# A decoder layer: 18 of the 22 gate and up tiles of both SwiGLUs computed in pairs by seven half-size block products

## The chip, the cores and the metric

One NeuronCore of a Trainium2 chip. TensorE (PE) multiplies a weight block of 128 x 128, which it loads first (PEld), with a moving tile of up to 512 columns and adds the products up in a PSUM bank; it has two clocks, 1.2 and 2.4 GHz. VectorE (DVE), ScalarE (ACT) and GpSimd (POOL) work on 128 partitions of SBUF or PSUM; SyncE (SP) issues the DMAs. The metric is the device time of one launch in microseconds, the median over runs.

## The reference

One layer on 512 tokens of 1024 features, all in float32:

```
h = x
h = h + 0.5 * rms(swiglu(rms(h, g1), Wgate1, Wup1, Wdown1), g1post)     # FFN1, d_ff = 2816
u = rms(h, gmix)
proj = u @ w_in                       # inputs of two token mixers and their gates
y_a = sparse latent attention(proj)   # top 128 keys per token, 8 heads
y_b = chunked gated linear recurrence(proj), 4 heads
merged = sigmoid(gate_a) * (y_a @ w_br_a) + sigmoid(gate_b) * (y_b @ w_br_b)
h = h + rms(merged @ w_out, gmixpost)
h = h + 0.5 * rms(swiglu(rms(h, g2), Wgate2, Wup2, Wdown2), g2post)     # FFN2, d_ff = 2816
h = h + rms(sigmoid(rms(h, gple) @ w_ple_gate) * (p @ w_ple_proj), gplepost)

swiglu(x) = (silu(x @ Wgate) * (x @ Wup)) @ Wdown
rms(x, g) = x * rsqrt(mean(x * x) + 1e-6) * g
```

## The kernel before

Activations lie transposed, features on partitions: `h` is 8 blocks of 128 features by 512 tokens. Every product is made in three parts, to keep float32 accuracy: an operand is cast to a shorter float (`hi`, ACT), the rest is `lo` = operand - `hi` (DVE), and PE adds `w_hi x hi`, `w_lo x hi` and `w_hi x lo` into one bank (`mm3_step`, L206 to L209; `matmul`, L239). For the inputs, `prenorm_tile` (L283, L284) writes `hg_hi` and `hg_lo`, which hold `h` times the gain; the factor per token, 1/rms, is left out of the product and multiplied into its result as `R` (`scaled`, L360).

An FFN has 22 tiles of 128 hidden features in `GROUPS` of 8, 7 and 7. For a tile, `weight` fetches 128 x 1024 weights of gate into a `raw` tile by a DMA on SP, and `weight_part` casts (L163, ACT) and subtracts (L165, DVE) into a `w` tile; likewise up. Each of the two products is 8 blocks of features x 3 parts = 24 matmuls of 512 tokens, into a bank of its own from a ring of eight (`mm`, `pl`, `hg`, `pt`, `po`). `hidden` then multiplies both by `R` on DVE (L360), takes silu on ACT, multiplies the two (L369, DVE) and splits into `hid_hi` (L186, ACT) and `hid_lo` (L187, DVE). After a group, eight down products use its hidden tiles (`product`): for m of the 8 output blocks, nf x 3 matmuls of 512 into a bank; the first group is copied to `y` (ACT), later ones are added (L413, DVE).

In FFN1 tile 0 is made while x arrives (`begin`). In FFN2 tiles 0 and 1 are computed in two halves of 256 tokens, since the second half's input is ready later. In the last group `last_product` computes the last 4 (FFN1) or 5 (FFN2) down blocks in token halves too, so that `residual` of the first half (post norm, sum, next pre-norm) runs beside the products of the second. Tiles are allocated from rings (`raw` 3, `w` 6, `t` 4 deep), and a scheduler orders each engine's instructions by estimated times; the kernel is otherwise written in program order.

POOL adds squares for the norms (L277), takes a few weight splits and parts of the mixers. In the gate and up products it has nothing to do.

## Time and profile before

| | us |
|---|---|
| median of 3 timed runs (lowest, highest) | 1249.57 (1249.42, 1252.25) |
| the profiled execution, its own time | 1253.45 |
| its span in the profile | 1251.7 |
| PE, DVE, ACT, POOL busy in the span | 1223.0, 710.7, 531.7, 297.7 |
| mean granted clock of PE (1 is the higher level) | 0.997 |

The stages, in us from the start of the span, read off the lines in the trace: FFN1 gate/up of its three groups 5 to 99.7, 143.3 to 220.3 and 258.4 to 334.5, each followed by its down products; residual to about 375; mixers and their input products to 735; merge to 822.6; FFN2 to 1192.8; the last part with the per-layer embeddings to 1251.7. Busy time is the union of an engine's instructions; a matmul's modelled duration overlaps the next one's, so the pitch is read between starts, not from durations.

### The profile page before, as it was taken

How to read it: one execution, taken by the hardware profiler on the slowest of the kernel's cores; microseconds unless marked ns; L12 is line 12 of the kernel's file. 1: busy time of each engine (PE TensorE's matmuls, PEld its weight loads, DVE VectorE, ACT ScalarE, POOL GpSimd, SP SyncE). 2: the span in 40 equal slices, each digit the busy share in tenths (PEclk: the TensorE clock that was granted, in tenths of full speed). 3: DMA queues.
4: the chain of work that ended last, by engine and by line, in shares of the span. 5: the costliest groups of instructions: out<-in, count | busy, mean ns of one | idle time of the engine just before them, and what ended most of it. 6: DMA issues, size and time to landing. Idle time of an engine off the chain costs nothing.

```text
span 1251.7 us, 16612 instructions
## 1 busy us (share of the span) xinstructions
PE 1223.0 (98%) x6263; PEld 1036.9 (83%) x6263; DVE 710.7 (57%) x1252; ACT 531.7 (42%) x909; POOL 297.7 (24%) x348
## 2 busy tenths in 40 slices
PE   7999999999999999999999999989999999999997
PEld 5888888888898888888878887988888888888986
DVE  7543226444448659997766758295532444444386
ACT  6423213222336455555767654364332222222363
POOL 3000000000045203636856622360000000000374
PEclk9999999999999999999999999999999999999999
DMA  6432354333245402423212245223323323332131
GB/s 223 134 94 93 89 107 130 111 101 93 78 129 171 142 21 85 128 89 122 72 55 87 91 146 191 76 85 101 115 87 101 99 88 100 101 95 91 51 152 68
DMA packets 45576, 131.29 MB, mean 105 GB/s; under 512 B 5144, under 2 KB 10424, under 8 KB 45496
## 3 DMA queue, kind: packets, MB, share of 16 engines
q1 hardware_dynamic: 45496, 130.24, 33.4%
q8 instruction: 49, 0.80, 0.3%
q14 instruction: 31, 0.25, 0.1%
HBM read 118.16 MB, written 12.06 MB: 104 GB/s over the span
## 4 chain that ended last, share of the span: by engine, by line
PE 80%; DVE 11%; ACT 3%; DMA 2%; issue 2%; POOL 1%; SPq 0%; DVEq 0%; POOLq 0%; ACTq 0%
PE mm L239 32%; PE pl L239 21%; PE po L239 10%; PE pt L239 9%; DVE hg_lo L284 2%; DVE w L165 2%; DVE h L338 1%; PE po L581 1%; DMA g<-gate_d 1%; DVE z L336 1%; PE hg L705 1%; DVE sc L532 1%; PE pl L560 1%; PE pt L577 1%; DVE small L531 1%
## 5 line engine op out<-in xcount | busy, mean ns | idle before, releaser
L163 ACT ACTIVATE w<-raw 128x1024 fp32r<-128x1024 f32 (+5 forms) x205 | 208.6, 1021 | 384.9 <-PE mm L239 111.7
L239 PE MATMUL mm<-hg_hi,w 128*128 128x512 f32 (+1 forms) x1104 | 339.9, 387 | 0.7 <-DVE small L569 0.7
L165 DVE TENSOR_TENSOR w<-raw,w 128x1024 fp32r<-128x1024 f32 (+5 forms) x189 | 228.6, 1213 | 105.3 <-ACT w L163 103.8
L239 PEld LDWEIGHTS mm<-hg_hi,w 128*128 128x128 f32 x1104 | 203.6, 188 | 40.2 <-DVE w L165 1.1
L277 POOL TENSOR_TENSOR acc<-acc,sq 128x256 f32<-128x256 f32 x78 | 68.0, 876 | 683.9 <-ACT sq L276 682.6
L239 PE MATMUL mm<-hg_lo,w 128*128 128x512 f32 (+1 forms) x552 | 212.6, 387 | 1.3 <-DVE hg_lo L284 1.3
L239 PE MATMUL pl<-hg_hi,w 128*128 128x512 f32 (+1 forms) x592 | 174.2, 377 | 5.3 <-ACT w L163 5.0
L239 PEld LDWEIGHTS pl<-hg_hi,w 128*128 128x128 f32 x592 | 108.8, 191 | 25.6 <-ACT w L163 5.0
L239 PEld LDWEIGHTS mm<-hg_lo,w 128*128 128x128 f32 x552 | 103.5, 188 | 21.3 <-DVE hg_lo L284 1.5
L239 PE MATMUL pl<-hg_lo,w 128*128 128x512 f32 (+1 forms) x296 | 110.3, 376 | 0.7 <-DVE hg_lo L284 0.7
L239 PE MATMUL pt<-hg_hi,w 128*128 128x512 f32 (+1 forms) x256 | 79.2, 388 | 0.8 <-ACT w L163 0.5
L239 PE MATMUL pl<-hid_hi,w 128*128 128x512 f32 (+1 forms) x290 | 79.0, 359 | 0.0
L360 DVE TENSOR_TENSOR t<-mm,R 128x512 f32<-128x512 f32 (+1 forms) x44 | 29.1, 662 | 86.5 <-PE mm L239 65.7
L239 PE MATMUL po<-hg_hi,w 128*128 128x512 f32 (+1 forms) x256 | 77.1, 382 | 0.0
L239 PE MATMUL mm<-hid_hi,w 128*128 128x512 f32 (+1 forms) x278 | 75.3, 357 | 0.0
L239 PEld LDWEIGHTS pl<-hg_lo,w 128*128 128x128 f32 x296 | 56.0, 191 | 10.6 <-DVE hg_lo L284 1.0
L239 PEld LDWEIGHTS pl<-hid_hi,w 128*128 128x128 f32 x290 | 51.7, 189 | 8.1
L239 PEld LDWEIGHTS pt<-hg_hi,w 128*128 128x128 f32 x256 | 47.9, 190 | 11.7 <-ACT w L163 1.0
L239 PEld LDWEIGHTS mm<-hid_hi,w 128*128 128x128 f32 x278 | 49.6, 189 | 7.6
L239 PEld LDWEIGHTS po<-hg_hi,w 128*128 128x128 f32 x256 | 47.5, 188 | 9.4
L360 DVE TENSOR_TENSOR t<-pl,R 128x512 f32<-128x512 f32 (+1 forms) x30 | 20.2, 672 | 58.6 <-PE pl L239 58.5
L239 PE MATMUL pl<-hid_lo,w 128*128 128x512 f32 (+1 forms) x145 | 52.0, 359 | 0.0
(300 smaller groups left out, 2144.4 us busy)
## 6 DMA issues: line engine op xcount, KB each, us to landing
raw<-ffn_w_gate SPq DMA_DIRECT2D x43, 512.0 KB, 3.6
raw<-ffn_w_up SPq DMA_DIRECT2D x43, 512.0 KB, 3.6
raw<-ffn_w_down SPq DMA_DIRECT2D x32, 448.0 KB, 3.3
raw<-ffn_w_down SPq DMA_DIRECT2D x16, 512.0 KB, 3.5
raw<-w_gates SPq DMA_DIRECT2D x16, 512.0 KB, 3.6
gate_d<-t SPq DMA_DIRECT2D x16, 256.0 KB, 2.0
raw<-w_br SPq DMA_DIRECT2D x8, 512.0 KB, 3.2
raw<-w_out SPq DMA_DIRECT2D x8, 512.0 KB, 4.3
```

Of the source, the lines that this page charges most:

```text
L163: hi = nc.scalar.activation(w[:, 0, c], raw[:, c], AF.Copy)
L165: lo = eng.tensor_tensor(w[:, 1, c], raw[:, c], w[:, 0, c].bitcast(F32), op=OP.subtract)
L239: i = self.nc.tensor.matmul(*args, **kw)
L277: eng.tensor_tensor(acc[:, c:c + 256], acc[:, c:c + 256], sq, op=OP.add)
L284: lo = nc.vector.scalar_tensor_tensor(self.hg_lo[:, k, cols], self.h[:, k, cols], g, self.hg_hi[:, k, cols].bitcast(F32), op0=OP.mult, op1 ...
L336: nc.vector.scalar_tensor_tensor(z, y[:, k, c], g[:, k:k + 1], bc, op0=OP.mult, op1=OP.mult)
L338: eng.tensor_tensor(self.h[:, k, c], self.h[:, k, c], z, op=OP.add)
L360: self.nc.vector.tensor_tensor(t, ps, self.R[:, cols], op=OP.mult)
L531: nc.vector.max(best, sc)
L532: nc.vector.match_replace(sc, best, sc, TAKEN)
L560: nc.tensor.matmul(pl, st[:, tok], kh[:, part, :nk], start=(part == 0), stop=(part == 1))
L577: nc.tensor.transpose(pt[:, k], lg[:, k], self.ident)
```

## The change

The weight tiles of nine pairs in each FFN (18 of the 22 tiles) are no longer multiplied one by one. For gate, and for up, the two tiles and the 8 feature blocks, as 2 x 2 blocks (A11, A12: the first tile's weights for the first four and the last four feature blocks; A21, A22: the second tile's), meet the input's 2 x 2 blocks (B: feature halves by token halves) in seven block products of 4 feature blocks x 256 tokens x 3 parts = 12 matmuls each, by the Strassen-Winograd scheme. It needs four sums of input blocks, T1 to T4, made once per FFN (`input_sums`: from `h` times gain, subtractions on POOL, split on ACT and DVE), and four sums of weight blocks per tile pair, S1 to S4 (`pair`: two on POOL, two on DVE, each split on ACT and DVE). Sums of results are made in PSUM where products share a bank (banks "a", "c") and otherwise by a copy out of PSUM (ACT) and an addition (DVE). `R` is multiplied into the gate half on POOL (`gated`) and into the product's second factor on POOL or DVE.

The groups are 6, 4, 6 and 6 tiles; the first has tiles 0 to 3 as before and one pair, the others two, three and three pairs. The down products are thus in four groups, and the first three blocks of a group are made in two steps: their products with all but the last two hidden tiles first, then those with the last two (`early`). `hid` is 6 tiles deep, `raw` five, `t` six; `w` tiles of pairs begin 16 columns into a tile with 64 columns more; `w_proj` shares its memory with T.

```diff
-GROUPS = ((0, 8), (8, 7), (15, 7))
+
+GROUPS = ((0, 6, 4), (6, 4, 0), (10, 6, 0), (16, 6, 0))
+INNER = 6
+SEVEN = (("a", True, "A11", "B11"), ("b", True, "A12", "B21"), ("a", False, "S2", "T2"), ("c", True, "S1", "T1"),
+         ("a", False, "S3", "T3"), ("c", False, "S4", "B22"), ("a", False, "A22", "T4"))
+SHIFT = 16
...
-        return self.wpool.tile([P, 1024], F32, tag="raw", name="raw", bufs=3)
-
-    def weight_tile(self):
-        return self.wpool.tile([P, 2, 1024], F32R, tag="w", name="w", bufs=6)
+        return self.wpool.tile([P, 1024], F32, tag="raw", name="raw", bufs=5)
+
+    def weight_tile(self, shift=0):
+        t = self.wpool.tile([P, 2048 + 64], F32R, tag="w", name="w", bufs=6)
+        return t[:, shift:shift + 2048].rearrange("p (a c) -> p a c", a=2)
...
-        return self.tmp.tile([P, NT], F32, tag="t", name="t", bufs=4)[:, :n]
+        return self.tmp.tile([P, NT], F32, tag="t", name="t", bufs=6)[:, :n]
...
-        for m in range(split):
+        for m in range(done, split):
...
-        hid_hi = pool.tile([P, 8, NT], F32R, name="hid_hi")
+        hid_hi = pool.tile([P, INNER, NT], F32R, name="hid_hi")
...
+            if first:
+                sums = self.input_sums(f"{name}_pre", pool)
+                next(sums)
-            for j in range(j0, nf):
+            for j in range(j0, plain):
...
+                next(sums, None)
+            if first:
+                for _ in sums:
+                    pass
+            for j in range(plain, nf, 2):
+                self.pair(pool, [src[f0 + j:f0 + j + 2] for src in (wg, wu)], hid_hi, hid_lo, j)
...
+            early = 3
+            ps = [self.bank() for _ in range(early)]
+            for ks in (range(nf - 2), range(nf - 2, nf)):
+                for m in range(early):
+                    parts(m, ps[m], FULL, ks)
+            for m in range(early):
+                store(m, ps[m], FULL)
...
+                self.last_product(product, y, acc, post, nxt, TURN[name], spill, early)
...
+    def input_sums(self, gname, pool):
+
+        nc = self.nc
+        self.T = [pool.tile([P, 2, 4, 256], F32R, tag="T", name=f"T{i}", bufs=4) for i in range(4)]
+        one, two = HALF
+        for k in range(4):
+            b1, b2 = self.t(), self.t()
+            for b, kk in ((b1, k), (b2, k + 4)):
+                nc.scalar.activation(b, self.h[:, kk, :], AF.Copy, scale=self.gain(gname)[:, kk:kk + 1])
+            s = self.sum_tile(pool).rearrange("p (i t) -> p i t", i=4)
+            for i, (x, z) in enumerate(((b1[:, two], b1[:, one]), (b2[:, two], s[:, 0]), (b2[:, two], b1[:, two]),
+                                        (b2[:, one], s[:, 1]))):
+                nc.gpsimd.tensor_tensor(s[:, i], x, z, op=OP.subtract)
+                self.split(self.T[i][:, 0, k, :], self.T[i][:, 1, k, :], s[:, i])
+            yield
...
+    def weight_parts(self, w, raw, eng):
+
+        self.nc.scalar.activation(w[:, 0], raw, AF.Copy)
+        eng.tensor_tensor(w[:, 1], raw, w[:, 0].bitcast(F32), op=OP.subtract)
...
+        last = self.weight_tile(SHIFT)
+        for i, src in enumerate(srcs):
+            r = [self.raw_tile() for _ in range(2)]
+            for x, z in zip(r, src):
+                nc.sync.dma_start(x, z)
+            w = [self.weight_tile(SHIFT) for _ in range(3)]
+            s = self.sum_tile(pool)
+            at = {"A11": (w[0], low), "A12": (w[0], high), "S1": (w[1], low), "S2": (w[1], high), "S3": (w[2], low),
+                  "A22": (w[2], high), "S4": (last, (low, high)[i])}
+            sides.append((r, w, s, {k: v[:, :, c] for k, (v, c) in at.items()}))
+        for r, w, s, at in sides:
+            self.weight_parts(w[0], r[0], dve)
+        for r, w, s, at in sides:
+            pool_.tensor_tensor(s[:, low], r[1][:, low], r[1][:, high], op=OP.add)
+            dve.tensor_tensor(s[:, high], s[:, low], r[0][:, low], op=OP.subtract)
+            self.weight_parts(w[1], s, dve)
+        for r, w, s, at in sides:
+            pool_.tensor_tensor(r[1][:, low], r[0][:, low], r[1][:, low], op=OP.subtract)
+            self.weight_parts(w[2], r[1], dve)
+        for r, w, s, at in sides:
+            dve.tensor_tensor(r[0][:, high], r[0][:, high], s[:, high], op=OP.subtract)
+            self.weight_parts(at["S4"], r[0][:, high], dve)
+        banks = [{}, {}]
+        kept = [{}, {}]
+        out = [[self.t() for _ in range(2)] for _ in range(2)]
+        def keep(i, name, bank, tag):
+            kept[i][name] = c = self.bt(256, tag, 2)
+            nc.scalar.copy(c, banks[i][bank])
+        def after(i, n):
+            b, k, (o1, o2) = banks[i], kept[i], out[i]
+            if n == 0:
+                keep(i, "P1", "a", "sq")
+            elif n == 1:
+                dve.tensor_tensor(o1[:, one], b["b"], k["P1"], op=OP.add)
+            elif n == 2:
+                keep(i, "U2", "a", "z")
+            elif n == 3:
+                keep(i, "P5", "c", "acc")
+            elif n == 4:
+                dve.tensor_tensor(o2[:, two], b["a"], k["P5"], op=OP.add)
+            elif n == 5:
+                dve.tensor_tensor(o1[:, two], b["c"], k["U2"], op=OP.add)
+                if i == 0:
+                    self.gated(o1)
+                else:
+                    self.inner(hid_hi, hid_lo, j, o1, out[0][0])
+            elif i == 0:
+                dve.tensor_tensor(o2[:, one], b["a"], self.R[:, one], op=OP.mult)
+                pool_.tensor_tensor(o2[:, two], o2[:, two], self.R[:, two], op=OP.mult)
+                self.gated(o2, True)
             else:
-                for m in range(KT):
-                    product(m, FULL)
+                dve.tensor_tensor(o2[:, one], b["a"], out[0][1][:, one], op=OP.mult)
+                self.inner(hid_hi, hid_lo, j + 1, o2, out[0][1], two)
+        for n, (bank, opens, wn, xn) in enumerate(SEVEN):
+            hi, lo = self.input_part(xn)
+            for i, (r, w, s, at) in enumerate(sides):
+                if opens:
+                    banks[i][bank] = self.bank()[:, :256]
+                ps, wt = banks[i][bank], at[wn]
+                for k in range(4):
+                    c = slice(k * P, (k + 1) * P)
+                    for q, (a, x) in enumerate(((0, hi), (1, hi), (0, lo))):
+                        self.matmul(ps, wt[:, a, c], x[:, k, :], start=(opens and k == 0 and q == 0),
+                                    stop=(k == 3 and q == 2), **({} if opens else {"skip_group_check": True}))
+                after(i, n)
+        for _ in range(2):
+            next(self.ring)
+    def gated(self, z, scaled=False):
+        nc = self.nc
+        if not scaled:
+            nc.gpsimd.tensor_tensor(z, z, self.R, op=OP.mult)
+        nc.scalar.activation(z, z, AF.Silu)
+        nc.gpsimd.tensor_tensor(z, z, self.R, op=OP.mult)
+    def inner(self, hid_hi, hid_lo, j, u, s, cols=FULL):
+        self.nc.vector.tensor_tensor(u[:, cols], u[:, cols], s[:, cols], op=OP.mult)
+        self.split(hid_hi[:, j, :], hid_lo[:, j, :], u)
...
-                                    [pool.tile([P, 2, 1024], F32R, name=f"w_proj{i}") for i in range(3)])
+                                    [pool.tile([P, 2, 1024], F32R, tag="T", name=f"w_proj{i}", bufs=4) for i in range(3)])
...
+    nc = bacc.Bacc("TRN2", target_bir_lowering=False, num_devices=1, dynamic_dma_scratch_size=1024)
```

Three places where instructions move. DVE in FFN1's first group, before, one tile (`mm`, `pl` are the banks of gate and up, `w<-raw,w` makes a weight's `lo`):

```order
L165 TENSOR_TENSOR w<-raw,w 128x1024
L187 TENSOR_TENSOR hid_lo<-t,hid_hi 128x512
L360 TENSOR_TENSOR t<-mm,R 128x512
L165 TENSOR_TENSOR w<-raw,w 128x1024
L360 TENSOR_TENSOR t<-pl,R 128x512
L369 TENSOR_TENSOR t<-t 128x512
L165 TENSOR_TENSOR w<-raw,w 128x1024
L187 TENSOR_TENSOR hid_lo<-t,hid_hi 128x512
```

After, DVE in FFN2's second group, part of a pair's work (`s` holds sums of weights, `po`, `mm`, `pl`, `pt` are results of block products, `sq_` and `acc_` copies of earlier ones):

```order
L514 TENSOR_TENSOR s<-s,raw 128x512
L536 TENSOR_TENSOR t<-po,sq_9361 128x256
L490 TENSOR_TENSOR w<-raw,w 128x512 x2
L536 TENSOR_TENSOR t<-mm,sq_9376 128x256
L490 TENSOR_TENSOR w<-raw,w 128x1024
L520 TENSOR_TENSOR raw<-raw,s 128x512
L514 TENSOR_TENSOR s<-s,raw 128x512
L490 TENSOR_TENSOR w<-raw,w 128x1024
L542 TENSOR_TENSOR t<-pl,acc_9447 128x256
L490 TENSOR_TENSOR w<-s,w 128x1024
```

A tile's two evictions, one product and one split stood between two weight splits of 1024; now the evictions are of 256, between sums (512) and splits of weights (1024).

DVE at the first pair of FFN2, before: the first whole tiles.

```order
L369 TENSOR_TENSOR t<-t 128x512
L165 TENSOR_TENSOR w<-raw,w 128x1024
L187 TENSOR_TENSOR hid_lo<-t,hid_hi 128x512
L360 TENSOR_TENSOR t<-mm,R 128x512
L369 TENSOR_TENSOR t<-t 128x512
L165 TENSOR_TENSOR w<-raw,w 128x1024
L360 TENSOR_TENSOR t<-pl,R 128x512
L187 TENSOR_TENSOR hid_lo<-t,hid_hi 128x512
```

After, the same place (`T_8642` to `T_8645` are T1 to T4, `L536` evicts the second block product, `L514` makes S2, `w<-s,w` splits S1 and S2):

```order
L196 TENSOR_TENSOR T_8642<-s,T_8642 128x256
L536 TENSOR_TENSOR t<-pl,sq_8910 128x256
L196 TENSOR_TENSOR T_8644<-s,T_8644 128x256
L196 TENSOR_TENSOR T_8643<-s,T_8643 128x256
L196 TENSOR_TENSOR T_8642<-s,T_8642 128x256
L196 TENSOR_TENSOR T_8644<-s,T_8644 128x256
L536 TENSOR_TENSOR t<-mm,sq_8925 128x256
L196 TENSOR_TENSOR T_8645<-s,T_8645 128x256
L196 TENSOR_TENSOR T_8643<-s,T_8643 128x256
L196 TENSOR_TENSOR T_8645<-s,T_8645 128x256
L514 TENSOR_TENSOR s<-s,raw 128x512
L520 TENSOR_TENSOR raw<-raw,s 128x512
```

The last six subtractions for T stand ahead of the first sum and split of the pair's weights; six more rows of T stand further up.

POOL, gate and up products of FFN1, before: from the last `r` of the input's norm to the first sum of squares of the down products there is nothing.

```order
L230 TENSOR_TENSOR r<-small_252,mhalf 128x2
L230 TENSOR_TENSOR r<-small_261,mhalf 128x2
L277 TENSOR_TENSOR acc_119<-acc_119,sq_2265 128x256
L277 TENSOR_TENSOR acc_119<-acc_119,sq_2268 128x256
L277 TENSOR_TENSOR acc_119<-acc_119,sq_2299 128x256
```

After (`s<-t` and `s<-t,s` are input sums, L513 and L517 sums of weights, L551, L576, L578 multiplications by R):

```order
L471 TENSOR_TENSOR s<-t 128x256
L513 TENSOR_TENSOR s<-raw 128x512
L471 TENSOR_TENSOR s<-t 128x256
L471 TENSOR_TENSOR s<-t,s 128x256
L517 TENSOR_TENSOR raw<-raw 128x512
L471 TENSOR_TENSOR s<-t,s 128x256
L513 TENSOR_TENSOR s<-raw 128x512
L517 TENSOR_TENSOR raw<-raw 128x512
L551 TENSOR_TENSOR t<-t,R 128x256
L576 TENSOR_TENSOR t<-t,R 128x512
L578 TENSOR_TENSOR t<-t,R 128x512 x2
```

The last input sums and the first pair's weight sums are mixed, and behind them come the pair's multiplications by `R`.

## Rows read from the trace of the kernel before

**Rows 1.** The page's first part, PE: busy us, share, instructions.
```profile
PE 1223.0 (98%) x6263; PEld 1036.9 (83%) x6263; DVE 710.7 (57%) x1252; ACT 531.7 (42%) x909; POOL 297.7 (24%) x348
```

**Rows 2.** Busy time by stretch: us, PE, PEld, DVE, ACT, POOL, PEclk, DMA share, GB/s.
```profile
22.00:99.70 77.70, 77.70 (x350) 64.52 (x351) 40.22 (x49) 28.19 (x35) 2.30 (x2) 1.00 0.42 129
99.70:143.30 43.60, 43.60 (x194) 35.85 (x193) 11.71 (x11) 12.52 (x16) 0.00 (x0) 1.00 0.31 94
...
400.00:735.00 335.00, 328.92 (x1835) 281.51 (x1835) 250.25 (x619) 198.93 (x393) 163.53 (x204) 0.99 0.28 89
822.60:853.00 30.40, 27.21 (x215) 25.86 (x215) 28.59 (x54) 18.10 (x41) 16.99 (x20) 1.00 0.23 69
...
1192.80:1251.70 58.90, 50.45 (x266) 42.05 (x264) 44.43 (x77) 27.23 (x62) 34.55 (x34) 0.99 0.27 103
...
410.70:414.00 3.30, 3.30 (x18) 3.30 (x17) 1.91 (x8) 1.75 (x6) 0.44 (x1) 0.53 0.02 6
```

**Rows 3.** PE's timeline, FFN1: start us, us, line, operation, shape, count, first and last.
```profile
301.89 0.62 PE L239 MATMUL pt<-hg_hi,w 128*128 128x512 f32 x2
...
306.65 0.62 PE L239 MATMUL pt<-hg_hi,w 128*128 128x512 f32 x2
```

**Rows 4.** PE's timeline, FFN2's start in halves of 256 columns, first and last.
```profile
846.57 0.40 PE L239 MATMUL mm<-hg_hi,w 128*128 128x256 f32 x2
...
849.09 0.28 PE L253 MATMUL hg<-ones,acc 128*128 128x1 f32 x2
```

**Rows 5.** DVE by line and shape, 143.3 to 334.5: count, busy us, mean ns, idle before.
```profile
L165 DVE TENSOR_TENSOR w<-raw,w 128x1024 fp32r<-128x1024 f32 x23 | 28.1, 1222 | 6.5 <-ACT w L163 6.5
...
L369 DVE TENSOR_TENSOR t<-t 128x512 f32<-128x512 f32 x13 | 9.0, 692 | 1.4
```

**Rows 6.** DVE's timeline: first use of R and last plain eviction, FFN1; first use, FFN2.
```profile
31.39 0.68 DVE L360 TENSOR_TENSOR t<-pl,R 128x512 f32<-128x512 f32 x1
...
56.34 0.69 DVE L360 TENSOR_TENSOR t<-po,R 128x512 f32<-128x512 f32 x1 [3.12 <-PE po L239]
...
857.02 0.42 DVE L360 TENSOR_TENSOR t<-pt,R 128x256 f32<-128x256 f32 x1 [0.96 <-ACT R L293]
```

**Rows 7.** ACT by line and shape: 143.3 to 334.5, then the whole span.
```profile
L163 ACT ACTIVATE w<-raw 128x1024 fp32r<-128x1024 f32 x23 | 24.3, 1058 | 83.8 <-DMA raw<-ffn_w_gate 23.0 <-PE mm L239 18.4 <-PE pl L239 15.2
...
L186 ACT ACTIVATE hid_hi<-t 128x512 fp32r<-128x512 f32 x13 | 8.2, 634 | 8.0 <-DVE t L369 8.0
...
L283 ACT ACTIVATE hg_hi<-h,vecs 128x256 fp32r<-128x256 f32 x48 | 24.1, 504 | 25.1 <-DVE h L338 23.6 <-POOL h L338 1.3
...
L579 ACT COPY at<-pt 128x256 f32<-128x256 f32 x8 | 2.9, 362 | 1.0 <-PE pt L577 1.0
```

**Rows 8.** POOL's additions, by tile: least, mean and most ns, when, shape.
```profile
L909 POOL TENSOR_TENSOR g<-g,g x8: 1288/1674/2299, 747.1 to 786.6; 128x512 f32<-128x512 f32 x8
...
L277 POOL TENSOR_TENSOR acc<-acc,sq x78: 721/754/1717, 347.7 to 1228.7; 128x256 f32<-128x256 f32 x78
```

**Rows 9.** DVE's and POOL's timelines in the mixers, three places.
```profile
460.37 0.48 DVE L515 SCALAR_TENSOR_TENSOR sc<-lg,wi,sc 128x256 f32<-128x256 f32 x1
...
468.51 2.46 DVE L515 SCALAR_TENSOR_TENSOR sc<-lg,wi,sc 128x256 f32<-128x256 f32 x1 [0.84 <-ACT lg L511]
468.29 2.40 POOL L165 TENSOR_TENSOR w<-raw,w 128x1024 fp32r<-128x1024 f32 x1 [36.93 <-ACT w L163]
...
487.70 0.68 DVE L485 TENSOR_TENSOR q<-mm,R 128x512 f32<-128x512 f32 x1
487.55 2.42 POOL L165 TENSOR_TENSOR w<-raw,w 128x1024 fp32r<-128x1024 f32 x1
```

**Rows 10.** PE's timeline, a wait in the mixers and one at the end.
```profile
408.77 0.33 PE L479 MATMUL pt<-ident,t 128*128 128x128 f32 x1 [1.87 <-DVE t L473]
...
1195.92 0.50 PE L239 MATMUL mm<-w,hg_lo 128*128 128x512 f32 x1 [1.32 <-DVE hg_lo L284]
```

**Rows 11.** The page's fifth part, weight loads: count, busy us, mean ns, idle before.
```profile
L239 PEld LDWEIGHTS mm<-hg_hi,w 128*128 128x128 f32 x1104 | 203.6, 188 | 40.2 <-DVE w L165 1.1
```

More of the change, by code (lines that the diff above doesn't have):

```diff
@@ L375, in ffn @@
         post = self.ghalf[f"{name}_post"]
-        hid_hi = pool.tile([P, 8, NT], F32R, name="hid_hi")
-        hid_lo = pool.tile([P, 8, NT], F32R, name="hid_lo")
+        hid_hi = pool.tile([P, INNER, NT], F32R, name="hid_hi")
+        hid_lo = pool.tile([P, INNER, NT], F32R, name="hid_lo")
         acc = self.accum(NT)
-        for f0, nf in GROUPS:
+        for f0, nf, plain in GROUPS:
             first, last = f0 == 0, f0 + nf == FT
@@ L401, in ffn, with parts, store @@
                 self.hidden(hid_hi, hid_lo, j, pg, pu, FULL)
+                next(sums, None)
[4 more added lines that the diff above has]
+                self.pair(pool, [src[f0 + j:f0 + j + 2] for src in (wg, wu)], hid_hi, hid_lo, j)
             w = {}
[L404 removed]
+            def parts(m, ps, cols, ks):
                 if m not in w:
                     w[m] = self.weight(wd[m][:, f0 * P:(f0 + nf) * P], nf * P)
[L407 to L409 removed]
+                for k in ks:
+                    self.mm3_step(k, ps, w[m], hid_hi, hid_lo, nf, cols)
+            def store(m, ps, cols):
                 if first:
@@ L415, in product @@
                     self.square_sum(acc[:, cols], y[:, m, cols], m == 0, nc.vector if m == KT - 1 else nc.gpsimd)
+            def product(m, cols):
+                ps = self.bank()[:, :cols.stop - cols.start]
+                parts(m, ps, cols, range(nf))
+                store(m, ps, cols)
+            early = 3
[3 more added lines that the diff above has]
+                    parts(m, ps[m], FULL, ks)
@@ L417, in ffn @@
+            for m in range(early):
+                store(m, ps[m], FULL)
             if last:
-                self.last_product(product, y, acc, post, nxt, TURN[name], spill)
+                self.last_product(product, y, acc, post, nxt, TURN[name], spill, early)
                 if begin:
                     self.ple_proj(pool)
-            elif first and begin:
-                for m in range(KT):
+            else:
+                for m in range(early, KT):
                     product(m, FULL)
-                begin[2]()
-            else:
-                for m in range(KT):
-                    product(m, FULL)
+                if first and begin:
+                    begin[2]()
@@ new lines, in sum_tile, with input_part @@
+    def sum_tile(self, pool):
+        return pool.tile([P, 1024], F32, tag="s", name="s", bufs=2)
+    def input_part(self, name):
+        if name[0] == "T":
+            t = self.T[int(name[1]) - 1]
+            return t[:, 0], t[:, 1]
+        k, c = (slice(4 * i, 4 * i + 4) for i in (int(name[1]) - 1,)), HALF[int(name[2]) - 1]
+        k = next(k)
+        return self.hg_hi[:, k, c], self.hg_lo[:, k, c]
+    def weight_parts(self, w, raw, eng):
+        self.nc.scalar.activation(w[:, 0], raw, AF.Copy)
+        eng.tensor_tensor(w[:, 1], raw, w[:, 0].bitcast(F32), op=OP.subtract)
@@ new lines, in pair @@
+    def pair(self, pool, srcs, hid_hi, hid_lo, j):
+        nc = self.nc
+        pool_, dve = nc.gpsimd, nc.vector
+        low, high = slice(0, 512), slice(512, 1024)
+        one, two = HALF
+        sides = []
+        last = self.weight_tile(SHIFT)
[42 more added lines that the diff above has]
+                    self.gated(o1)
+                else:
+                    self.inner(hid_hi, hid_lo, j, o1, out[0][0])
[3 more added lines that the diff above has]
+                self.gated(o2, True)
+            else:
+                dve.tensor_tensor(o2[:, one], b["a"], out[0][1][:, one], op=OP.mult)
[14 more added lines that the diff above has]
+            next(self.ring)
```

8 lines of the change are left out of this document (2 added, 6 removed).

## The prediction

> **What bounds the kernel now.** I read the busy shares first: TensorE's queue (PE) is busy 98% of the span [rows 1]. A busy PE can still be a waiting PE, so next comes the table by stage: in the gate, up and down products of both FFNs PE's busy time equals the stretch, at full clock, with no wait for any engine [rows 2]. There the time is the count of matmuls times their pitch, and an engine beside PE is worth nothing until PE waits for it. PE waits only at the edges: in the mixers (328.92 of 335.00 us busy), at the second FFN's start (27.21 of 30.40) and in the last 59 us (50.45 of 58.90). Third, the pitch, from PE's timeline: 21 matmuls of 512 columns start in 306.65 - 301.89 = 4.76 us, 226.7 ns each [rows 3]; 21 of 256 columns, each with another weight block, start in 849.09 - 846.57 = 2.52 us, 120.0 ns each [rows 4]. Halving the columns costs 13 ns a matmul.
>
> **The products.** A pair of tiles, gate and up, is 4 x 8 x 3 = 96 matmuls of 512 columns now: 96 x 226.7 = 21.76 us. By seven block products it is 2 x 7 x 4 x 3 = 168 of 256 columns: 168 x 120.0 = 20.16 us. Fewer columns (12.5%), but 72 matmuls more, so 1.60 us a pair; nine pairs in two FFNs: 18 x 1.60 = 28.8 us off the path. The down products keep their 22 x 8 x 3 matmuls an FFN; eight evictions more (a fourth group, 0.69 each on DVE [rows 5]) lie beside PE.
>
> **What the other engines must do in a pair's 20.16 us.** Durations from [rows 5 to 8]. ACT: six casts of 1024 (1.06), two of 512 (0.63), six copies of 256 out of PSUM (0.36), two silus and two casts (0.63): 12.3 us. DVE: six subtractions of 1024 (1.22), nine operations of 512 (0.69), nine of 256 (0.42): 17.3 us. POOL: seven of 512 (1.29 at the least) and one of 256 (0.75): 9.8 us; it had nothing there. Each fits alone. DVE and POOL together may not. A DVE operation with two SBUF inputs that began 0.22 us after a POOL one of 2.40 us took 2.46 us where its like took 0.48: it ended 0.28 us after POOL did, so it waited for all of it [rows 9]. POOL waits in turn: the same addition of 512 takes 1.29 to 2.30 us [rows 8]. A DVE operation that reads PSUM is not held: 0.68 us inside a POOL operation of 2.42 [rows 9]. Of a pair's 17.3 us on DVE 8 x 0.42 = 3.4 read PSUM; 13.9 lock. 13.9 + 9.8 = 23.7 us by the records, 3.6 above PE's 20.16, if nothing overlaps; below, nothing at all, if POOL's work falls where DVE idles (20.16 - 17.3 = 2.9 us) or reads PSUM.
> The Trainium skill's "SBUF — State Buffer", section "Who interferes with whom", says that a VectorE instruction with two SBUF inputs and a GpSimd instruction that reads SBUF exclude each other for the whole of one instruction; the row shows just that, and by the rule every later pair would be paced at 23.7 us.
> The first pair of a group has its weights made during the down products before it, where DVE is busy 11.71 of 43.60 us and POOL not at all [rows 2]. So 0 + 1 + 2 + 2 pairs of an FFN's groups, ten in all, are made beside another pair. Within such a run PE has slack: the bank that DVE empties after product five is written again three blocks later (3 x 12 x 0.120 = 4.3 us). Two cycles that each lose 3.6 overrun it by 2.9, one does not: 4 x 2.9 = 11.6 us. Ends 0 and 36 us; I take 2.0, nearest the slack, because half of POOL's work waits for product results and so falls between DVE's.
>
> **The first pair of each FFN.** The four input sums are new work: 16 subtractions of 256 on POOL (0.75), 16 casts of 256 and eight of 512 on ACT (0.50, 0.63), 16 subtractions of 256 on DVE (0.42) [rows 6 to 8]. They need the finished input, and the last of them stand ahead of the sums of weights on POOL and DVE (the order rows in the section on the change). FFN2: R's second half is there at 857.0 (DVE's first use [rows 6]); PE begins the plain tiles at 853.0 [rows 2] and reaches the third block product after two tiles and two block products: 853.0 + 96 x 0.2267 + 48 x 0.120 = 880.5. Into these 23.5 us DVE must put, up to the weights of S1, eleven operations of 512, 26 of 256 and one of 1024: 7.6 + 10.9 + 1.2 = 19.7 us. Ten of them read PSUM (four of 512, six of 256, 5.3 us), so 14.4 lock. POOL must put in 16 x 0.75 + 2 x 1.29 = 14.6. Together 29.0, 5.5 too many: I take a wait of 5. FFN1: from 31.4 (R's first use) to 56.3 (the eviction behind the last plain tile [rows 6]) + 5.8 = 62.1, so 30.7 us for 16.0 of locking on DVE (ten of 512, 16 of 256, two of 1024) and 15.9 on POOL (16 x 0.75 + 3 x 1.29): 1.2 us too many, and the chain from the last tile's silu through sum, cast and subtraction to S1 ends about 1.3 later: 2.5 us. An idle PE also loses its clock: after 1.87 us of idle at 408.77 [rows 10] the stretch 410.70 to 414.00 had a granted clock of 0.53 [rows 2], close to the lower of its two levels, 1.2 and 2.4 GHz; 3.3 us at half give 1.6 away. I add 1.5 for FFN2. Together 9.0 us; ends 3 (only FFN2's, half of it) and 19.
>
> **From a pair to the down products.** The last pair's second tile passes through DVE, silu, POOL, DVE, a cast and DVE: 0.42 + 0.62 + 1.29 + 0.42 + 0.42 + 0.63 + 0.69 = 4.5 us after block 13 ends, 3.1 after PE's last block; with one lock and one queued weight split (1.2 each) 5.5. Three banks of down products on the tiles before cover 3 x 4 x 3 x 0.2267 = 8.2 us in a group of six, 4.1 in the group of four. Two groups of four, 1.0 each: 2.0 (0 to 4).
>
> **The last group.** It has six tiles, not seven, so the second half of the down products shrinks from 84 to 72 matmuls (FFN1) and 105 to 90 (FFN2): 1.44 + 1.80 us less cover for the first half's residual. PE already waits for that chain (1.32 us at 1195.92 [rows 10]), so little of it is free: 2.5 (0 to 3.2).
>
> **The mixers** are untouched, but five raw tiles instead of three and six scratch tiles instead of four let the scheduler order them anew. PE idles 6.1 us there; a new order can win some or lose as much: 1.0 (-3 to +6).
>
> **Sum.** -28.8 + 9.0 + 2.0 + 2.0 + 2.5 + 1.0 = -12.3 us. The profiled execution took 1253.45 us (span 1251.7 and 1.75 around it), so its like would take 1241.1. The median of the timed runs, 1249.57, is 3.9 lower: 1237.
>
> **Rivals.**
> (1) DVE and POOL exclude each other and the pairs run at their pace: slower. For it: [rows 9], and 23.7 against 20.16. Against: the slack, and that DVE idles 43.60 - 11.71 = 31.9 us in the down products ahead of a group [rows 2]. The place is the ten later pairs; with 14.5 us lost elsewhere it decides from (28.8 - 14.5) / 10 = 1.4 us a pair; at 3.0 (3.6 less the slack's part) it is +15.7: 1265. 17%.
> (2) Only the products count: sums and locks hide, the first pair of FFN2 costs 3, the tails 1.5: -24.3, 1225. For it: PE's order holds every later pair in plain sequence. Against: the sum of rows for the first pair. 15%.
> (3) The first pairs eat it: the sums come 6 us late in FFN1 and 10 in FFN2, each with 1.7 of lost clock: 19.4 + 7.5 = 26.9, 1248. For it: DVE and POOL at 29.0 against 23.5 us. Against: in FFN1 POOL was busy 2.30 of 77.70 us [rows 2]. 13%.
> (4) It does not do what it says, since each matmul of 256 waits for its weight load of 188 ns [rows 11]: 31.6 us a pair, 1427. [Rows 4] all but exclude it: 120 ns with a load each. 1%.
>
> **Numbers.** The forecast has 54%, its own range 1229 to 1245. Over 0.3% (3.7 us, about what a measurement of this kernel tells from no change) faster: nearly all of it, (2) and a third of (3), 72%; within: 10%; slower: most of (1), 18%. The range 1222 to 1262 holds the forecast, (3), most of (2) and the nearer half of (1).
>
> **What would show it.** Right: 168 matmuls start in about 20.2 us in the middle pairs; waits of PE at the first pair, for T or the weights of S1, longer in FFN2; in the groups of four a wait for hid_lo. DVE subtractions of 1024 over 1.6 us beside POOL. Wrong: middle pairs over 21.8 us with PE waiting for a DVE eviction or a weight (rival 1); no wait over 1 us in the first pairs (rival 2); a pitch of 256 columns over 125 ns with T or shifted weights; over 8 us more idle in the mixers.

## The result: slower by 2.4%

The changed kernel took 1280.98 us (median of 4 runs, 1276.73 to 1282.41) against 1250.76 for the kernel before, measured beside it: a ratio of 1.0236, 95% interval 1.0207 to 1.0265. The forecast was 1237. Its profiled execution took 1276.73 us with a span of 1274.9, its fastest run, and that of the kernel before, 1253.45, was slower than any of its timed runs. So the spans of the two profiles are 23.2 us apart where the medians are 30.2 apart; the 23.2 are what is divided up below.

First part of the page of the changed kernel, as [rows 1]:

```profile
PE 1196.0 (94%) x7532; PEld 1068.4 (84%) x7532; DVE 926.4 (73%) x1532; ACT 644.9 (51%) x1155; POOL 547.8 (43%) x524
```

PE is busy 27 us less, and the span is 23 us longer: some 50 us of new waits. Busy time by stretch, columns as in [rows 2]: FFN1's gate and up products of the first, second, third and fourth group; mixers and merge; FFN2's first, second, third and fourth group; the last part.

```profile
5.08:80.29 75.21, 70.33 (x377) 59.76 (x378) 60.90 (x84) 45.71 (x80) 32.73 (x33) 1.00 0.42 147
113.56:179.41 65.85, 41.81 (x337) 41.32 (x337) 28.90 (x40) 19.40 (x34) 15.99 (x11) 0.79 0.40 78
201.20:264.82 63.62, 60.30 (x505) 59.63 (x504) 54.40 (x66) 31.59 (x52) 27.85 (x19) 0.97 0.34 108
297.49:358.63 61.14, 59.86 (x505) 59.45 (x504) 52.00 (x64) 31.75 (x52) 28.88 (x19) 1.00 0.35 111
394.29:845.48 451.19, 436.56 (x2487) 373.49 (x2486) 324.80 (x729) 264.25 (x511) 207.72 (x249) 1.00 0.32 105
845.48:928.29 82.81, 71.29 (x481) 65.68 (x480) 64.96 (x109) 45.78 (x94) 38.86 (x43) 0.94 0.19 62
960.95:1000.53 39.58, 39.58 (x338) 39.57 (x336) 28.74 (x39) 20.13 (x35) 15.92 (x11) 1.00 0.30 94
1022.31:1085.98 63.67, 60.30 (x506) 59.56 (x504) 54.46 (x66) 31.56 (x52) 28.79 (x19) 1.00 0.34 108
1118.64:1178.84 60.20, 59.09 (x506) 58.69 (x504) 51.72 (x64) 31.70 (x52) 28.63 (x19) 1.00 0.35 114
1214.23:1274.90 60.67, 51.54 (x264) 42.14 (x264) 44.78 (x78) 28.04 (x66) 35.85 (x34) 0.98 0.23 83
```

The two groups of two pairs (second of FFN1, second of FFN2) have the same 336 matmuls. One takes 39.58 us without a wait, 19.79 a pair; the other takes 65.85. The mixers took 448.21 before (374.60 to 822.81), the last part 58.90 [rows 2]. The largest wait, by PE's, ACT's and SP's timelines (start us, us, what; in brackets the idle time ahead and what ended it):

```profile
151.29 0.58 PE L248 MATMUL pl<-hg_hi,w 128*128 128x256 f32 x1 [22.49 <-ACT acc L529]
...
149.93 1.06 ACT L489 ACTIVATE w<-raw 128x1024 fp32r<-128x1024 f32 x1 [26.15 <-DMA raw<-ffn_w_up]
...
114.30 0.79 SPq L157 DMA_DIRECT2D bias_d<-t  x1
115.76 14.31 SPq L504 DMA_DIRECT2D raw<-ffn_w_up  x2
```

PE waits for a PSUM bank that ACT is to copy out; ACT, whose queue is in order, stands at the cast of a weight, and the weight is on its way. It was asked for at 115.76 us, right behind `bias_d<-t`, the write of a bias table for the mixers (1536 KB), which the change doesn't touch. The kernel before has the same (SP and ACT):

```profile
144.75 0.79 SPq L149 DMA_DIRECT2D bias_d<-t  x1
146.21 8.25 SPq L162 DMA_DIRECT2D raw<-ffn_w_gate  x1
...
180.41 1.06 ACT L163 ACTIVATE w<-raw 128x1024 fp32r<-128x1024 f32 x1 [23.03 <-DMA raw<-ffn_w_gate]
```

From the write's issue to the first cast of a weight behind it: 35.7 us before, 35.6 after. Before, PE did not wait all the same. Eight weights of the group had been asked for ahead of the write; each feeds PE for 24 matmuls, 5.4 us, and PE came to the ninth, the one cast at 180.41, only at 187.66. DVE stood too, for a scratch tile that the write still read, but the eight products had banks enough (PE, first and ninth product; DVE):

```profile
144.00 0.50 PE L239 MATMUL pt<-hg_hi,w 128*128 128x512 f32 x1
...
187.66 0.39 PE L239 MATMUL mm<-hg_hi,w 128*128 128x512 f32 x1
...
179.13 0.69 DVE L360 TENSOR_TENSOR t<-mm,R 128x512 f32<-128x512 f32 x1 [20.68 <-DMA bias_d<-t]
```

So before, PE could run on for 43 us behind the write's issue. In the changed kernel it ran on for 14.5 us, to 128.80. The weights of the pair that it was in were there; but within a pair PE writes a bank again after ACT has copied it out, and in ACT's queue the cast of the next pair's up weight stands ahead of that copy.

### The profile page after: what moved, and what is told of

Read it like the earlier page. It is cut to its first block, busy times and chain, and to the rows that moved or that the text cites. A ratio compares the mean times of both kernels' runs of the same rounds, so it can differ in the third digit from the quotient of the medians.

```text
span 1274.9 us, 19983 instructions
## 1 busy us (share of the span) xinstructions
PE 1196.0 (94%) x7532; PEld 1068.4 (84%) x7532; DVE 926.4 (73%) x1532; ACT 644.9 (51%) x1155; POOL 547.8 (43%) x524
## 4 chain that ended last, share of the span: by engine, by line
PE 55%; DVE 25%; issue 8%; ACT 5%; POOL 4%; DMA 3%; SPq 0%; DVEq 0%; POOLq 0%; ACTq 0%
PE mm L248 21%; PE pl L248 15%; PE pt L248 6%; PE po L248 6%; DVE w L490 5%; DVE w L174 2%; DVE hg_lo L293 2%; DVE sc L687 2%; DVE h L347 2%; DVE z L345 1%; DVE small L686 1%; DMA g<-gate_d 1%; PE po L736 1%; DVE s L514 1%; DMA raw<-ffn_w_gate 1%
## 5 line engine op out<-in xcount | busy, mean ns | idle before, releaser
L248 PE MATMUL mm<-hg_hi,w 128*128 128x512 f32 (+1 forms) x984 | 268.1, 355 | 3.4 <-ACT hg_hi L195 1.5
L172 ACT ACTIVATE w<-raw 128x1024 fp32r<-128x1024 f32 (+5 forms) x149 | 135.1, 913 | 87.2 <-PE mm L248 24.4
L174 DVE TENSOR_TENSOR w<-raw,w 128x1024 fp32r<-128x1024 f32 (+5 forms) x133 | 146.9, 1112 | 38.2 <-ACT w L172 37.7
L490 DVE TENSOR_TENSOR w<-raw,w 128x1024 fp32r<-128x1024 f32 (+1 forms) x108 | 146.1, 1368 | 19.3 <-ACT w L489 19.3
L513 POOL TENSOR_TENSOR s<-raw 128x512 f32<-128x512 f32 x36 | 52.5, 1459 | 220.2 <-DMA raw<-ffn_w_gate 110.2
L248 PE MATMUL pl<-hg_hi,w 128*128 128x256 f32 (+1 forms) x504 | 111.7, 314 | 27.6 <-ACT acc L529 22.5
L489 ACT ACTIVATE w<-raw 128x1024 fp32r<-128x1024 f32 (+1 forms) x108 | 95.6, 912 | 61.1 <-DMA raw<-ffn_w_up 26.1
L248 PE MATMUL mm<-T,w 128*128 128x256 f32 x552 | 74.2, 284 | 7.7 <-DVE t L542 4.3
L248 PE MATMUL pl<-hg_lo,w 128*128 128x256 f32 (+1 forms) x252 | 77.6, 311 | 0.7 <-DVE hg_lo L293 0.7
L514 DVE TENSOR_TENSOR s<-s,raw 128x512 f32<-128x512 f32 x36 | 32.3, 896 | 63.1 <-POOL s L513 63.1
L248 PEld LDWEIGHTS mm<-T,w 128*128 128x128 f32 x552 | 68.8, 192 | 9.2 <-DVE t L542 5.1
L248 PE MATMUL pl<-T,w 128*128 128x256 f32 x540 | 72.3, 283 | 3.9 <-ACT w L489 2.0
L578 POOL TENSOR_TENSOR t<-t,R 128x512 f32<-128x512 f32 x36 | 59.2, 1647 | 25.9 <-ACT t L577 25.8
```

Source lines behind the costliest of these rows:

```text
L172: hi = nc.scalar.activation(w[:, 0, c], raw[:, c], AF.Copy)
L174: lo = eng.tensor_tensor(w[:, 1, c], raw[:, c], w[:, 0, c].bitcast(F32), op=OP.subtract)
L248: i = self.nc.tensor.matmul(*args, **kw)
L489: self.nc.scalar.activation(w[:, 0], raw, AF.Copy)
L490: eng.tensor_tensor(w[:, 1], raw, w[:, 0].bitcast(F32), op=OP.subtract)
L513: pool_.tensor_tensor(s[:, low], r[1][:, low], r[1][:, high], op=OP.add)
```

## The experiments

**The write of the bias table.** Four places for it. First, called behind FFN1's tile 0:

```
             begin[1]()
             self.hidden(hid_hi, hid_lo, 0, *ps, FULL)
+            begin[2]()          # bias_vector; the call behind the first group goes
```


> The changed kernel with the bias table (its product, its write of 1536 KB to DRAM) made right behind FFN1's tile 0, when the DMA queue is idle, not behind the first group's down products. Theory: the 22.5 us wait of PE at 126.9 to 149.4 us in the second group of FFN1 is the up weights of a pair, queued behind that write; it and 2.2 us of lost clock go, all other waits stay: about 25 us less than the changed kernel, 1252 to 1258 us. Rival: the pair's seven weight tiles are fetched too late in any case, because the rings (5 raw tiles, 6 weight tiles) are short of a pair's need; then a wait of over 10 us stays in that group and the time is above 1270.

1281.09 us. The second group now took 39.74 us without a wait, but two waits stood in the first group, 15.72 us and 9.13. The first, and what ACT, and DVE behind it, stood for:

```profile
76.67 0.58 PE L248 MATMUL pl<-hg_hi,w 128*128 128x256 f32 x1 [15.72 <-DVE t L369]
...
72.83 0.63 ACT L376 ACTIVATE t<-t 128x512 f32<-128x512 f32 x1 [30.67 <-DMA bias_d<-t]
```

ACT's silu waits there for a scratch tile that the write, issued at 38.40, still reads: the table's row lies in one of the six and holds it while it is written. That suggested another cause for the wait in the changed kernel. So, the place as in the change and a tile of its own; and, the place as in the change and ACT as the issuer:

```
-        bv = self.t(BVEC)[:HEADS]
+        bv = c.tile([HEADS, BVEC], F32, name="bv")
---
-        nc.sync.dma_start(self.bias_d, ...)      # "..." as before
+        nc.scalar.dma_start(self.bias_d, ...)
```


> The changed kernel with the bias table's row in a tile of its own, not in one of the six scratch tiles, written to DRAM at the same place as in the changed kernel (the paddings of the weight tiles shrink from 64 to 16 columns to make room). In the run with the table early, PE waited behind a scratch tile. If the write's hold on a scratch tile is also what stops FFN1's second group, the wait of 22.5 us goes and the time is 1252 to 1260 us. If the weights wait in the DMA queue behind the write, nothing changes: 1275 to 1284 us.

> The changed kernel with the write of the bias table issued by ACT instead of SP, at the same place of the program. If the weights waited because they stood behind the write in one queue, they pass it now, and the time is that of the bias table made early, 1252 to 1258 us. If they waited because the write holds the DMA engines themselves, whatever queue it is in, the wait stays at 15 us or more: above 1270.

A tile of its own: 1285.09 us, PE waits 20.24 us; in the changed kernel the scratch tile is not it. From ACT's queue: 1267.68 us, between the two expectations:

```profile
137.13 0.58 PE L248 MATMUL pl<-hg_hi,w 128*128 128x256 f32 x1 [6.45 <-ACT acc L529]
```

ACT's cast of the up weight came 19.6 us behind the write's issue, not 35.6. So the queue is most of the wait, and a part is left when weights can pass. Last, the row in a part of `y` that is not yet in use, and the write issued when the first group's weights are in:

```
-        onehot = self.t(BVEC)[:32]
+        onehot = y[:32, KT - 2, :BVEC]
-        bv = self.t(BVEC)[:HEADS]
+        yield                         # the rest behind tile 1 of the first group
+        bv = y[:HEADS, KT - 1, :BVEC]
```


> The bias table made in FFN1's first group, its row in a part of y that is written only later (no scratch tile is held), its write issued when all gate and up weights of that group are in and the DMA queue is idle. Theory (the weights of the second group queue behind the write): its 24.6 us go without a new wait, FFN1's second group takes 39.7 us: 1252 to 1260 us. Rival (the rings are too short for pairs in any case, or the write collides with whatever stands behind it): a wait of over 8 us elsewhere in FFN1, above 1265.

1253.93 us (ratio 1.0023, 1.0006 to 1.0039). FFN1's second group, and a stretch in which only the write is under way (last two columns: DMA share, GB/s):

```profile
114.20:154.42 40.22, 39.86 (x338) 39.65 (x337) 28.92 (x39) 19.91 (x35) 15.65 (x11) 1.00 0.31 94
...
45.00:55.00 10.00, 10.00 (x46) 8.29 (x45) 5.60 (x10) 5.80 (x11) 4.79 (x6) 1.00 0.45 49
```

The stall is gone, and 27 us with it. The write keeps 45% of the DMA engines busy at 49 GB/s, so 1536 KB take some 32 us. The Trainium skill, "DMA: Bandwidth & Descriptors", section "Rules for kernel authors", says that an outermost dimension of fewer than 16 confines a DMA to at most as many engines; the table's is 8 heads, and 45% is near 8 of 16. No run tried the 128 rows outermost. The Trainium skill, "DMA: Bandwidth & Descriptors", section "Issuing engines are not separate DMA queues", says that DMAs of several issuers interleave on the same engines, and that issuing from several saves only issue time. The 6.45 us that are left agree with the first; the 16 us that went do not agree with the second.

**DVE and POOL.** POOL's sums and its multiplications by R left out of the pairs, on the first kernel with the table early; then, on the last, POOL doing them into a tile that nobody reads:

```
-            pool_.tensor_tensor(s[:, low], r[1][:, low], r[1][:, high], op=OP.add)
+            # left out; S1 reads r[1]          (first kernel)
+            pool_.tensor_tensor(self.scr, r[1][:, 0:480], r[1][:, 512:992], op=OP.add)   # second
```


> The bias table early, and POOL's work in the pairs left out: the two sums of weights per side and the multiplications by R (gate half and factor), so the output is not the reference's; DVE's and ACT's instructions keep their count and sizes, only a sum's inputs are others. Theory (DVE and POOL exclude each other and pace the later pairs): the 10.9 us lost in later pairs go, and some 4 us of the first pairs' waits: 14 us less than with the bias table early. Rival (the later pairs wait for DVE's own load or for a ring of tiles): the losses stay, within 3 us of it.

> The bias table as in the run that splits it, and POOL doing its work of the pairs (480 of 512 columns, sums and multiplications) into a tile that nobody reads; DVE and ACT read what stood there before, so the output is not the reference's. Nobody waits for POOL's results, but POOL still reads SBUF beside DVE. If the exclusion of DVE and POOL is what the later pairs lose, they lose it here too: within 5 us of the kernel with the table split. If it is the chain through POOL (sum, then DVE, ACT, DVE), the time is 15 to 25 us less, as with POOL's work left out.

(The second run also takes the padding of the weight tiles from 64 to 16 columns, to make room.) 1256.71 us, 24.4 under its base; and 1268.85, 14.9 over its own. FFN1's third group, without POOL's work and with work for nobody:

```profile
199.30:258.66 59.36, 59.36 (x506) 59.36 (x505) 42.63 (x65) 33.11 (x53) 0.00 (x0) 1.00 0.36 116
...
178.95:245.44 66.49, 61.13 (x506) 60.51 (x505) 55.11 (x67) 31.37 (x51) 26.00 (x18) 0.97 0.30 104
```

Without POOL, six tiles take 3 x 19.79 = 59.36 us and DVE is busy 42.63; with POOL beside it DVE needs 55.11 for as many instructions. No result of POOL's is used there, so a loss needs no chain through POOL: the exclusion of [rows 9] is enough. Its path in that run is another one, though. PE's largest wait in each of the four groups of three pairs, 4.1 to 4.5 us and 17.0 together, is for a bank behind ACT's cast of a down weight; in FFN1's third group the DMA of that weight waited for DVE, which had worked nearly without a break since 217 us (PE, ACT, SP, DVE):

```profile
239.71 0.58 PE L250 MATMUL pl<-hg_hi,w 128*128 128x256 f32 x1 [4.21 <-ACT acc L533]
238.56 0.84 ACT L174 ACTIVATE w<-raw 128x768 fp32r<-128x768 f32 x1 [7.93 <-DMA raw<-ffn_w_down]
235.25 6.69 SPq L173 DMA_DIRECT2D raw<-ffn_w_down  x7
233.25 1.98 DVE L176 TENSOR_TENSOR w<-raw,w 128x768 fp32r<-128x768 f32 x1
```

PE's waits for an eviction by DVE in these four groups were 9.0 us in the changed kernel and 2.2 here, so this run does not say how much of the changed kernel's loss is the exclusion alone and how much the chain beside it. The changed kernel's trace shows the exclusion in single instructions ahead of the longest of these waits (PE; then DVE and POOL, start and us):

```profile
241.25 2.83 PE L248 MATMUL mm<-T,w 128*128 128x256 f32 x12 [2.10 <-DVE t L542]
...
240.78 0.41 DVE L542 TENSOR_TENSOR t<-mm,acc 128x256 f32<-128x256 f32 x1
...
236.36 1.66 DVE L520 TENSOR_TENSOR raw<-raw,s 128x512 f32<-128x512 f32 x1
237.95 1.77 DVE L514 TENSOR_TENSOR s<-s,raw 128x512 f32<-128x512 f32 x1
...
235.68 1.80 POOL L513 TENSOR_TENSOR s<-raw 128x512 f32<-128x512 f32 x1 [2.57 <-DMA raw<-ffn_w_up]
237.56 1.62 POOL L517 TENSOR_TENSOR raw<-raw 128x512 f32<-128x512 f32 x1
```

The operations of 512 take 1.7 us on DVE instead of 0.69 [rows 5], and DVE, busy from 231.88 on, comes late to the eviction. A part is the chain: L514 needs POOL's sum, which ended at 237.48. Had it begun then and run its 0.69 us, the eviction would have come some 1.5 us earlier, an estimate from these rows; that part of the 2.10 is the exclusion.

**The first pair.** All six tiles of the first group plain (`GROUPS = ((0, 6, 6), ...)`, table early); two of four input sums on DVE; the input sums in parts of `y` instead of the ring of two tiles `s` that the sums of weights use too:

```
-                nc.gpsimd.tensor_tensor(s[:, i], x, z, op=OP.subtract)
+                (nc.vector if i % 2 == 0 else nc.gpsimd).tensor_tensor(s[:, i], x, z, op=OP.subtract)
---
-            s = self.sum_tile(pool).rearrange(...)
+            s = y[:, 2 + k % 2 * 2:4 + k % 2 * 2, :].rearrange(...)
```


> The bias table early, and the first group of each FFN without a pair: six plain tiles, then groups of 4, 6, 6 in pairs (16 of 22 tiles). Theory: the 15.3 us that the first pairs lose (waits for T and the first weight sums, and their lost clock) go, against 2 x 1.94 us of gain given up: 11 us less than with the bias table early. Rival: the sums come late because POOL and DVE are too slow for them, and the wait moves to the first pair of the second group: 0 to 4 us more.

> The bias write split, and two of the four input sums (T1, T3) subtracted on DVE instead of POOL. If the first pair waits because the first weight sums stand behind 16 input sums in POOL's queue, FFN2's 8.3 us of waiting fall to under 4 and FFN1's 3.6 to under 2: 1247 to 1250 us. If it is DVE and POOL together, which exclude each other, a subtraction moved from the one to the other saves only its excess (8 x 0.33 = 2.6 us): 1251 to 1253 us. If it is something else (ACT's casts, the transfers), 1254 us.

> The bias write split, and the input sums before their split held in parts of y that are written only later, so that the sums of weights have their ring of two tiles for themselves. Theory: the first pair waits because its first weight sums need a tile that the last input sums still hold, and so come behind all of them, whichever engine adds; then FFN2's 8.3 us and FFN1's 3.6 us of waiting fall to under 2 each, with 2.5 us of lost clock: 1242 to 1246 us. Rival: DVE and POOL have too much to do in that stretch in any order; then T is late instead of the weights, and the wait stays over 6 us: 1251 to 1254 us.

Plain: 1262.14 us; FFN2's first group, behind its start, and the one after it had no wait over 1 us, but in FFN1 PE waited 4.33 us, while the write held a scratch tile again, and 8.62 us behind DVE, which stood for a sum of POOL's. Two sums on DVE: 1255.09, against 1253.93 without. PE at the third block product of FFN2, with the write split alone, with two sums on DVE, and with the sums apart:

```profile
885.31 0.58 PE L249 MATMUL po<-T,w 128*128 128x256 f32 x1 [5.76 <-ACT w L492]
```
```profile
887.13 0.58 PE L249 MATMUL po<-T,w 128*128 128x256 f32 x1 [6.96 <-ACT w L492]
```
```profile
894.79 0.39 PE L249 MATMUL po<-T,w 128*128 128x256 f32 x1 [1.50 <-DVE T L197]
```

Less work for POOL changed nothing; a ring of its own ended the wait for weights, and T became the last to come, 1.50 us late. POOL's row in the changed kernel says the same, its first sum of weights waits for one of DVE's last splits of T, which frees the tile:

```profile
904.68 2.93 POOL L513 TENSOR_TENSOR s<-raw 128x512 f32<-128x512 f32 x2 [3.30 <-DVE T L196]
```

Yet the run took 1260.22 us: in FFN1 the new order cast a down weight behind the bias write (issued at 45.99), and ACT and with it PE (9.24 us) stood again:

```profile
81.27 0.84 ACT L173 ACTIVATE w<-raw 128x768 fp32r<-128x768 f32 x1 [13.32 <-DMA raw<-ffn_w_down]
```

35.3 us behind the write's issue, like the 35.7 and 35.6 above. The two runs in which S1 does not pass through a tile `s` say the same of the first pair: PE's longest wait in FFN2's was 1.36 us without POOL's work and 1.33 with work for nobody.

**The surroundings.** The change's groups, rings and split down products, all tiles plain (`GROUPS = ((0, 6, 6), (6, 4, 4), (10, 6, 6), (16, 6, 6))`, no input sums); one more down block in halves (`TURN` 4 to 5 and 5 to 6); the deeper rings in the FFNs alone (tags `raw` 3 and `raw2` 2, `t` 4 and `t2` 2, the second of each used in `ffn` only), on the split write:

> The changed kernel's groups (6, 4, 6, 6), rings, split down products and bias write, but every tile multiplied as before, without pairs and without input sums: the change's surroundings alone. Theory: the mixers' new order and the shorter last halves cost 3 + 3 us, and the bias write, with 16 us of weights in the six weight tiles ahead of it, costs 0 to 3: 1255 to 1260 us. Rival (the write stops PE by its place among the shorter groups, pairs or not): over 1270.

> The kernel with the bias write split, and one more down block computed in halves in each FFN's last group (5 and 6 blocks, 90 and 108 matmuls in the second half instead of 72 and 90). Theory: the shorter cover costs 3 us of the change, and most of it comes back: 2 to 3 us less than with the write split alone, 1250 to 1252 us. Rival: the last part's 1.9 us come from the new order, not from the cover; then no gain, and 0.2 us more for each block in halves.

> The bias write split, and the deeper rings kept for the FFNs alone: outside them only three raw tiles and four scratch tiles are used, as in the kernel before. If the deeper rings made the new order of the mixers that takes 4 us more, these come back: 1249 to 1251 us. If it is something else that the change left in the mixers (the tile's width, the shared memory of T, where the FFN ends), 1253 to 1255 us.

Plain: 1261.74 us (ratio 1.0076), no wait behind the write, though it stands at its place in the change, mixers 452.45 us, last part 60.72. So it takes the pairs for the write to stop PE; and against this kernel the one with pairs and the write split, 1253.93, is 7.8 us faster. Half blocks: 1259.53, 5.6 more; PE waited 3.85 us at the last part's start, and the theory fell (the mixers' order moved too, with waits of 2.65 and 3.02 us). Rings: 1265.30; the mixers were 8.6 us faster than with the write split alone, FFN1 was 11 slower and FFN2 8 (their order changed too):

```profile
379.90:823.72 443.82, 435.13 (x2487) 373.98 (x2486) 323.39 (x729) 262.92 (x510) 212.79 (x249) 1.00 0.33 107
```

The rings with the sums apart took 1266.76.

> Both: the input sums held apart, and the deeper rings for the FFNs alone. If both theories hold, 1238 to 1242 us, faster than the kernel before by 0.8 to 1.1%; if only the first, 1242 to 1246; if only the second, 1248 to 1252.

**Towards a better version.** FFN2, or both FFNs, in five groups (`(0, 4, 4), (4, 4, 0), (8, 4, 0), (12, 4, 0), (16, 6, 0)`):

> The table's write early and behind the last up weights of FFN1's first group, and five groups an FFN: 4 plain tiles, then 4, 4, 4 and 6 tiles in pairs, nine pairs as in the change. Theory: groups of two pairs lose nothing (39.7 us each), the input sums have a whole group of down products more, so the first pairs lose nothing; left are the last group's 1.5 us each, the shorter last halves (3) and the mixers (3): 34.9 us of gain less 9, 26 us under the kernel before, 1223 to 1232 us. Rival (the sums and locks move with the pairs): above 1245.

> The bias write split, the one more block in halves, and FFN2 in five groups (4 plain, then 4, 4, 4 and 6 in pairs), which lost 7.5 us less than four groups in the run with five groups in both FFNs: 1253.9 - 7.5 - 2.5 = 1244 us, 1240 to 1248, faster than the kernel before by 0.3 to 0.9%. Rival: five groups gained by FFN1's delay, not by themselves; 1250 or more.

> The bias write split and FFN2 in five groups, the last halves as in the change: the run with one more block in halves without that block, whose last part took 4.5 us more and whose mixers 2.5 more. 1251.6 - 7 = 1244.5 us, 1242 to 1249, faster than the kernel before by 0.2 to 0.8%. Rival: the order of the mixers changes again and takes it away; 1250 to 1255.

Both: 1265.49; the write stood in FFN1's way again (8.37 us), but FFN2 took 362.5 us, against 369.9 with the write split alone. With one more block in halves: 1251.58, no difference from before. Without that, the write split and FFN2 in five groups: 1247.38 us, ratio 0.9956 (0.9943 to 0.9969), faster than both kernels. On it, scratch tiles and raw tiles deeper in the FFNs alone:

> The same, with six scratch tiles in the FFNs alone and four outside them. If the scratch tiles make the mixers' order that takes 4 us more than before, the mixers take 444 to 448 us instead of 452: 1237 to 1244 us if the FFNs' order stays, more if it changes. If it is the raw tiles, the mixers stay at 452.

> The same, with five raw tiles in the FFNs alone and three outside them, six scratch tiles everywhere. If the raw tiles make the mixers' order, the mixers take 444 to 448 us instead of 452; if the scratch tiles, 452.

1247.51 and 1249.45 us. Mixers and merge of these two:

```profile
369.86:822.05 452.19, 439.46 (x2487) 376.29 (x2486) 324.41 (x729) 264.27 (x511) 208.11 (x249) 0.99 0.33 105
```
```profile
378.26:824.71 446.45, 436.80 (x2487) 375.62 (x2486) 323.61 (x729) 262.40 (x510) 212.01 (x249) 1.00 0.33 107
```

So it is the five raw tiles, not the six scratch tiles, that made the mixers' new order. Three give 6 us back there; FFN1 lost as much.

## Why the prediction was wrong

| step | predicted | measured, by the stretches |
|---|---|---|
| products, 18 pairs | -28.8 | -36.3 |
| first pairs | 9.0 | 15.3 |
| later pairs, DVE and POOL | 2.0 | 11.2 |
| pair to down products | 2.0 | 0 |
| last group | 2.5 | 2.4 |
| mixers | 1.0 | 4.1 |
| bias write ahead of weights | none | 26.3 |
| sum | -12.3 | +23.0 |

Each is a stretch after less its like before. A pair before is 2 x 76.33 / 7 = 21.81 us (seven tiles), now 19.79. The first groups are set against 94.65 and 95.74 us less 23.83 (two tiles fewer, one pair); the others against 19.79 a pair. The last group's 2.4 are 1.8 of the last part and 0.6 in FFN2's stretch of down products and residual, against a tile's less. FFN1's like stretch took 1.1 us more, but that is work of the mixers' stretch: five matmuls with `w_proj`, which all stood behind 374.60 before, moved ahead into it.

```profile
391.01 1.33 PE L248 MATMUL mm<-w_proj,w_proj 128*128 128x512 f32 x5
```

So the mixers have 3.0 + 1.1. The write's 26.3 are 22.5 and 1.6 us of PE's waits, and nearly all the rest a granted clock of 0.50 in the 4.2 us from 149.40, the lower of the two levels.

**The step that failed** is one that the sum did not have: a transfer. The prediction counted what DVE, ACT and POOL must do in a pair and read from [rows 2] that the FFNs wait for nothing. It never asked how long the weights ahead of PE last, and did not look at SP's queue; the trace of before has a cast that waits 23.03 us for a weight in FFN1's second group, idle time that was covered, since PE had work and banks for 43 us. [Rows 7] has these 23.0 us, on ACT's cast. The change took the cover down to 14.5 us: PE now needs ACT within each pair, and ACT stood. With the write out of the way the kernel is 2.9 us slower than before, not 30. That is still not the forecast: FFN2, where no such write stands, gained 1.3 us in the changed kernel (368.75 against 370.01).

**Products**: right in kind; 117.8 ns a matmul, not 120.0 [rows 4].

**Later pairs**: the place was right, the size was not. The groups of two pairs lost nothing, those of three lost 4.3, 1.8, 4.3 and 0.8 us, as the text placed it. It worked out 4 x 2.9 = 11.6 us and then took 2.0, "because half of POOL's work waits for product results and so falls between DVE's". It does not fall between: 11.2 us were lost, near the 11.6. That the loss needs POOL's work is shown, and that the exclusion alone makes one; its share beside the chain through POOL's sums is open. Rival 1 gave this mechanism the place and 30 us; it had 11.

**First pairs**: the place and the wait for S1's weights were right, the reason was not. They lost 4.4 us in FFN1 and 10.9 in FFN2, where 2.5 and 6.5 were forecast. The sum of DVE's and POOL's work (29.0 against 23.5 us) is not what holds it: with work moved between them the wait stayed, with the ring left to the sums of weights it fell to 1.50 us. The ring of two was in the code. FFN2 gained only 1.2 us by that up to its second group (116.1 to 114.9): with the input sums made earlier, PE waited 2.71 us, not 0.62, for `hg_lo` at the start, and then ran at a granted clock of 0.61 for 4 us (1.00 without).

**Last group and mixers**: the last group came out as forecast, 2.4 us against 2.5; the mixers lost 4.1, not 1.0, inside the range that was given (-3 to +6). Without a pair the surroundings cost 7.6 us of span. The mixers' part came from the five raw tiles. That the shorter last halves are what the last group lost by is not shown: longer ones made it worse.

All four rivals were about engines; none had a transfer, and so the range ended at 1262.
